# Key search in a sparse-attention mixer: one fp32r pass per head over stacked high and low parts, scored ahead of compression

## Chip, cores and metric

The kernel runs on one core of one Trainium2 chip. The metric is the device time of one execution in microseconds; a comparison takes the median of several runs. The inputs and the output are in the chip's HBM, and everything between is one launch.

## What is computed

Two transformer blocks follow one another on 256 tokens of width 1024. The first is a feed-forward layer, a mixer of two kinds of attention, and a second feed-forward layer. The second block has two layers, each of them feed-forward, hybrid mixer, feed-forward. The hybrid mixer joins three attentions: stick-breaking (SB), NSA (compressed, selected and window keys), and DSA, a sparse attention in which a small index network picks the keys of each query. The change is in that key search:

```
iq = apply_rope(iq, cos_i, sin_i)                 # (S, 8 heads, 32)
ik = apply_rope(ik, cos_i, sin_i)                 # (S, 32), one for all heads
iw = iw * 8 ** -0.5 * 32 ** -0.5                  # (S, 8)
logits = relu(einsum('bthd,bsd->bths', qi, ik))
score = einsum('bths,bth->bts', logits, wi)       # -inf where s > t
_, idx = top_k(score, 64)                         # S // 4
# then softmax attention of each query over the 64 keys found
```

All of it is in fp32, with S = 256 tokens, handled as two halves of 128 (t = 0 and t = 1). Half 0 sees 128 keys, half 1 sees 256. In half 0 the mask of visible keys and the top 64 apply to the same 128 keys.

## The kernel before

**Projections.** Every large product is made of three fp32r passes (`mm3`, L255 to L257): weights and activations are split into a high part (rounded to fp32r) and a low part (the residual), and high x high, high x low and low x high are summed in PSUM. A weight tile of 128 x 1024 is fetched by SP's queue, its high part made by ScalarE (`hi`, L239) and its low part by VectorE (`lo`, L240); there are four buffers of each of `raw`, `hi` and `lo`. One such tile feeds 12 matmuls of 512 columns, six for each half of the tokens.

**Order.** The program is written in order, and a scheduler sets the order on each engine: of what is ready, what stands first in the program goes first, and a tile waits for a free buffer of its tag. Each engine then runs its list in order. In PSUM the tag `mm` has three banks (projections), `at` two (scores of every kind), `tp` two (transposes), `po` one.

**The hybrid mixer (`mixer2`)** runs in this order of program text: SB attention; `ckv`, the projections of NSA keys and values; `nq`, NSA queries; `ix`, the projection of the key search (296 columns: 8 heads x 32 of queries, 32 of keys, 8 weights); `dsaq`, the projection for the sparse attention; `cmp`, the compression of NSA keys and values, whose matmuls (L1189) read weights that lie split in the buffers `gl`; `nsa`, twelve units of NSA attention in a chain of scores, softmax, transposes and values, with the sparse attention of each half behind it; then `gate`, the gate projections (24 weight tiles, 288 matmuls), which write into the same `gl` buffers. The gate projections need nothing of the attentions, so they run as filler from the end of `dsaq` on.

**The key search.** `idx_evac` (L1076) takes each half's projection out of PSUM, applies rope, copies the key part four times beside itself (`kd`), makes three 128 x 128 transposes into one `tp` bank (L1086), and copies the queries (ScalarE, L1087) and keys (VectorE, L1088) to SBUF. `iq` then holds four heads in each of two column blocks, head b of a block on partitions 32b to 32b + 31, and `ik` holds the keys four times, once on each of these strips. `best(t)` (L1121) makes the scores: for each head an fp32 matmul over the 32 partitions of its strip (L1133; each shows as two records in the trace), two heads to an `at` bank, relu on ScalarE (`rl`, L1136), and on VectorE the sum over the heads weighted by `wi` (`iacc`, L1139). Then eight rounds find the eight largest of what is left and mark them (L1144, L1145), and the marks become the mask `M[t]` of the sparse attention.

`best` is a generator: the code of the compression and of the NSA units calls `step(n)`, which runs it on to its next `yield`, so that its parts are woven into theirs. Before, the first `step` (behind the compression's first eight matmuls) issues the scores of half 0 with the first round, and the scores of half 1 come when half 0 is done, among the NSA units.

Of the kernel before, what the change touches and what calls it, by code (L numbers as in the profile page):

```python
# [8 lines left out]
F32 = mybir.dt.float32  # L9
F32R = mybir.dt.float32r  # L10
# [6 lines left out]
P = 128  # L17
S = 256
# [99 lines left out]
class K:  # L118
# [732 lines left out]
    def mixer2(self, l, nxt):  # L851
        nc, tc, d = self.nc, self.tc, self.d
# [6 lines left out]
        with ExitStack() as outer:  # L859
# [3 lines left out]
            T = lambda shape, tag, bufs=1, dt=F32: self.tile(mp, shape, tag, dt, bufs)  # L863
            L = lambda shape, tag, bufs=1, dt=F32: self.tile(kp, shape, tag, dt, bufs)
            toks = [slice(0, P), slice(P, S)]
# [4 lines left out]
            for t in range(2):  # L870
                a = rsv[:, 2 * t:2 * t + 1]
                nc.vector.tensor_scalar(out=a, in0=xs[t][2], scalar1=0.125, scalar2=None, op0=OP.mult)
                b = rsv[:, 2 * t + 1:2 * t + 2]
# [4 lines left out]
            I = T  # L878
# [46 lines left out]
            r = self.rows([G("nsa_q_norm"), G("nsa_k_norm"), G("dsa_q_norm"), G("dsa_k_norm")])  # L925
            r = r.rearrange("p (i d) -> p i d", d=64)
# [17 lines left out]
            for s in range(2):  # L944
                hs = slice(64 * s, 64 * s + 64)
                nsp, zs = [], []
# [23 lines left out]
                for b in range(2):  # L970
                    nc.tensor.matmul(flat(R[b]), self.negl, flat(nsp[b][0]), start=True, stop=False)
                    nc.tensor.matmul(flat(R[b]), cb["identb"], cb[f"smask{b}"][:, :2 * (S - b * P)],
                                     start=False, stop=False)
# [6 lines left out]
                for t in range(2):  # L980
                    for r in range(2):
                        h = 2 * r + s
                        v = lambda b: sbv[b][:, 64 * h:64 * h + 64]
# [85 lines left out]

            self.sec = "ix"  # L1070

            iq = I([P, 2, S], "zs", 2)
            ik = I([P, 2, S], "zs", 2)[:, 0]
            wi = I([P, 2, 8], "wi")
            wi = [wi[:, t] for t in range(2)]

            def idx_evac(t, ps):
                tok = T([P, 296], "tok", 3)
                self.scaled(tok, ps, xs[t][2])
                self.rope(tok[:, :288].rearrange("p (g d) -> p g d", d=32), *cs(t, 8), 4)  # L1080
                nc.vector.tensor_scalar(out=wi[t], in0=tok[:, 288:296], scalar1=0.0625, scalar2=None, op0=OP.mult)
                kd = I([P, 4, 32], "kd", 2)
                nc.vector.tensor_copy(kd, tok[:, 256:288][:, None, :].to_broadcast([P, 4, 32]))
                p = self.tp([P, 3, P])
                for i, v in enumerate((tok[:, 0:P], tok[:, P:2 * P], kd.rearrange("p r d -> p (r d)"))):
                    nc.tensor.transpose(p[:, i], v, self.ident)  # L1086
                nc.scalar.copy(iq[:, :, toks[t]], p[:, 0:2])  # L1087
                nc.vector.tensor_copy(ik[:, toks[t]], p[:, 2])  # L1088

            self.proj(xs, w, 2456, 296, idx_evac)  # L1090
            self.sec = "dsaq"

# [30 lines left out]
            def best(t):  # L1123
                nk = P * (t + 1)
                vis, invis = c["vis"][:, S - nk:], c["invis"][:, S - nk:]
                acc = I([P, nk], f"iacc{t}")
                lgs = [self.at((P, 2, nk)) for _ in range(4)]
                first = True
                for b0 in range(0, 4, 2):
                    for r in range(2):  # L1130
                        for b in range(b0, b0 + 2):
                            bs = slice(32 * b, 32 * b + 32)
                            nc.tensor.matmul(lgs[b][:, r], iq[bs, r, toks[t]], ik[bs, :nk], start=True, stop=True)  # L1133
                    for b in range(b0, b0 + 2):
                        rl = I([P, 2, nk], "rl", 2)
                        nc.scalar.activation(rl, lgs[b], AF.Relu)  # L1136
                        for r in range(2):
                            h = 4 * r + b
                            nc.vector.scalar_tensor_tensor(out=acc, in0=rl[:, r], scalar=wi[t][:, h:h + 1],  # L1139
                                                           in1=invis if first else acc, op0=OP.mult, op1=OP.add)  # L1140
                            first = False
                for r in range(8):
                    m8 = self.sm(8, "m8")
                    nc.vector.max(out=m8, in_=acc)  # L1144
                    nc.vector.match_replace(out=acc, in_to_replace=m8, in_values=acc, imm_value=MARK)  # L1145
                    yield
                nc.vector.scalar_tensor_tensor(out=acc, in0=acc, scalar=MARK, in1=vis, op0=OP.is_equal, op1=OP.mult)
                m = T([P, nk], f"M{t}", 1, BF)
                nc.vector.tensor_scalar(out=m, in0=acc, scalar1=-1.0, scalar2=-NEG, op0=OP.add, op1=OP.mult)
                M[t] = m  # L1150

            side = [best(0), best(1)]

            def step(n):
                keep, self.sec = self.sec, "top"
                for _ in range(n):
                    while side:
                        try:
                            next(side[0])
                            break  # L1160
                        except StopIteration:
                            side.pop(0)
                self.sec = keep
# [3 lines left out]
            p = self.tp([P, 32])  # L1167
# [4 lines left out]
            for v in range(2):  # L1172
# [4 lines left out]
                for a in range(2):  # L1177
# [10 lines left out]
                    for m in range(8):  # L1188
                        nc.tensor.matmul(hp, ox[:, m].rearrange("p i c -> p (i c)"), w1[16 * v + 8 * a + m],  # L1189
                                         start=a == m == 0, stop=a == 1 and m == 7)  # L1190
# [4 lines left out]
                p = self.tp((P, 32))  # L1195
# [8 lines left out]
                if v == 0:  # L1204
# [3 lines left out]
                    kd = I([32, 2, 64], "kd", 2)  # L1208
                    nc.vector.tensor_copy(kd, kc[:32].to_broadcast([32, 2, 64]))
                    p = self.tp((P, 32))  # L1210
# [261 lines left out]
```

## Time and profile before

| what | value |
|---|---|
| median of 3 runs | 1759.06 us (1758.68 to 1761.39) |
| the profiled execution | 1758.43 us |
| its span, first to last instruction | 1756.6 us |
| TensorE busy in the span | 1735.0 us (99%) |
| VectorE busy | 1112.9 us (63%) |
| ScalarE busy | 933.8 us (53%) |
| GpSimd busy | 42.3 us (2%) |
| granted TensorE clock, mean | 0.999 |

Busy times of TensorE cover the whole of each matmul, also the part of it that lies under the next one; the step from the start of one matmul to the start of the next is what a matmul costs in a stream. The names in the trace are tile tags with the section that made them, so `lo_gate` is the low part of a gate weight and `at_top` a bank of key-search scores. Times of the views are counted from the span's start. The first hybrid mixer's part from `ix` to `nsa` lies at about 770 to 900 us, the second's 619 us later.

### The profile page before, as it was taken

Reading aid. Unit: us, or ns where it says so; the run is one execution under the profiler, and the core shown is the slowest. Engines: PE = TensorE matmul, PEld = TensorE weight load, DVE = VectorE, ACT = ScalarE, POOL = GpSimd, SP = SyncE. Lnnn points to the kernel's source line nnn. Section 1 sums busy time; section 2 is a strip of 40 time slices with the busy share of each in tenths; the row PEclk is TensorE's granted clock in tenths of the full one; section 3 lists DMA queues with packets and bytes.
Section 4 is the critical chain, followed back from the end, with each engine's and each line's share of the span. In section 5 each row is a group of like instructions: output and inputs, shape, how many; then the busy total and the mean of one; then the engine's idle time right before and its main releaser. Section 6 shows DMA issues by size and latency. Waiting matters only on the chain.

```text
span 1756.6 us, 22927 instructions
## 1 busy us (share of the span) xinstructions
PE 1735.0 (99%) x8461; PEld 1429.4 (81%) x8467; DVE 1112.9 (63%) x1800; ACT 933.8 (53%) x1458; POOL 42.3 (2%) x77
## 2 busy tenths in 40 slices
PE   9999999999999999999999999999999999999999
PEld 6888787788878888887887888888888877888887
DVE  5555677555565555697886555555556978875553
ACT  5444567544454454676655444444446766554442
POOL 0000200000000000100000000000001000000000
PEclk9999999999999999999999999999999999999999
DMA  8665644466556656554335665666556452357653
GB/s 286 184 190 182 206 133 144 134 190 183 190 180 197 186 182 202 182 151 146 94 108 187 199 190 181 203 180 185 186 193 205 135 160 85 104 172 206 187 183 132
DMA packets 151744, 303.97 MB, mean 173 GB/s; under 512 B 10584, under 2 KB 42368, under 8 KB 151632
## 3 DMA queue, kind: packets, MB, share of 16 engines
q1 hardware_dynamic: 150400, 301.61, 55.9%
q8 instruction: 67, 1.10, 0.3%
q10 hardware_dynamic: 592, 0.53, 0.1%
q0 software_dynamic: 640, 0.37, 0.1%
q14 instruction: 45, 0.37, 0.1%
HBM read 301.41 MB, written 1.05 MB: 172 GB/s over the span
## 4 chain that ended last, share of the span: by engine, by line
PE 90%; DVE 6%; ACT 2%; issue 1%; DMA 1%; POOL 0%; SPq 0%; DVEq 0%; ACTq 0%; POOLq 0%
PE mm_ffn L257 11%; PE mm_ffn L256 11%; PE mm_ffn L255 11%; PE at_ffn L257 9%; PE at_ffn L255 9%; PE at_ffn L256 9%; PE mm_gate L256 2%; PE mm_gate L257 2%; PE mm_gate L255 2%; PE tp_ffn L293 1%; PE po_ffn L293 1%; PE mm_m L255 1%; PE mm_m L257 1%; PE mm_m L256 1%; PE mm_ckv L257 1%
## 5 line engine op out<-in xcount | busy, mean ns | idle before, releaser
L240 DVE TENSOR_TENSOR lo_ffn<-raw_ffn,hi_ffn 128x1024 fp32r<-128x1024 f32 x392 | 478.1, 1225 | 451.5 <-ACT hi_ffn L239 450.1
L239 ACT CAST hi_ffn<-raw_ffn 128x1024 fp32r<-128x1024 f32 x392 | 411.1, 1054 | 499.9 <-PE at_ffn L257 307.0
L255 PE MATMUL mm_ffn<-hi_ffn,xh_ffn 128*128 128x512 f32 x288 | 112.3, 391 | 1.7 <-ACT xh_ffn L337 1.0
L256 PE MATMUL mm_ffn<-lo_ffn,xh_ffn 128*128 128x512 f32 x288 | 112.3, 391 | 1.1 <-DVE lo_ffn L350 1.1
L257 PE MATMUL mm_ffn<-hi_ffn,xl_ffn 128*128 128x512 f32 x288 | 112.2, 390 | 0.0
L256 PE MATMUL mm_ffn<-lo_ffn,ah_ffn 128*128 128x512 f32 x264 | 103.8, 393 | 0.0
L255 PE MATMUL mm_ffn<-hi_ffn,ah_ffn 128*128 128x512 f32 x264 | 103.3, 391 | 0.0
L256 PE MATMUL at_ffn<-lo_ffn,ah_ffn 128*128 128x512 f32 x264 | 103.1, 390 | 0.0
L257 PE MATMUL at_ffn<-hi_ffn,al_ffn 128*128 128x512 f32 x264 | 102.9, 390 | 0.0
L255 PE MATMUL at_ffn<-hi_ffn,ah_ffn 128*128 128x512 f32 x264 | 102.8, 389 | 0.0
L257 PE MATMUL mm_ffn<-hi_ffn,al_ffn 128*128 128x512 f32 x264 | 102.8, 389 | 0.0
L255 PE MATMUL at_ffn<-hi_ffn,xh_ffn 128*128 128x512 f32 x240 | 94.5, 394 | 0.0
L257 PE MATMUL at_ffn<-hi_ffn,xl_ffn 128*128 128x512 f32 x240 | 93.5, 390 | 0.0
L256 PE MATMUL at_ffn<-lo_ffn,xh_ffn 128*128 128x512 f32 x240 | 93.4, 389 | 0.0
L256 PE MATMUL mm_gate<-lo_gate,xh_ffn 128*128 128x512 f32 x192 | 78.5, 409 | 0.0
L257 PE MATMUL mm_gate<-hi_gate,xl_ffn 128*128 128x512 f32 x192 | 77.1, 405 | 0.0
L255 PE MATMUL mm_gate<-hi_gate,xh_ffn 128*128 128x512 f32 x192 | 77.0, 401 | 0.0
L256 PE MATMUL mm_ffn<-lo_ffn,xh_wo 128*128 128x512 f32 x192 | 74.9, 390 | 0.0
L257 PE MATMUL mm_ffn<-hi_ffn,xl_wo 128*128 128x512 f32 x192 | 74.8, 389 | 0.0
L255 PE MATMUL mm_ffn<-hi_ffn,xh_wo 128*128 128x512 f32 x192 | 74.7, 389 | 0.0
L255 PEld LDWEIGHTS mm_ffn<-hi_ffn,xh_ffn 128*128 128x128 f32 x288 | 54.1, 188 | 13.7 <-ACT hi_ffn L348 1.5
L256 PEld LDWEIGHTS mm_ffn<-lo_ffn,xh_ffn 128*128 128x128 f32 x288 | 54.1, 188 | 12.8 <-DVE lo_ffn L350 1.7
(632 smaller groups left out, 3996.6 us busy)
## 6 DMA issues: line engine op xcount, KB each, us to landing
raw_ffn<-in_ffn_w_gu_dram SPq DMA_DIRECT2D x160, 512.0 KB, 3.8
raw_ffn<-in_ffn_w_down_dram SPq DMA_DIRECT2D x132, 512.0 KB, 3.2
raw_gate<-in_w_gate_dram SPq DMA_DIRECT2D x48, 512.0 KB, 3.7
raw_ffn<-in_ffn_w_gate_dram SPq DMA_DIRECT2D x40, 512.0 KB, 3.8
raw_ffn<-in_ffn_w_up_dram SPq DMA_DIRECT2D x40, 512.0 KB, 3.7
raw_m<-in_w_in_dram SPq DMA_DIRECT2D x22, 512.0 KB, 4.2
raw_ffn<-in_ffn_w_gu_dram SPq DMA_DIRECT2D x32, 256.0 KB, 3.3
raw_wo<-in_w_out_dram SPq DMA_DIRECT2D x16, 512.0 KB, 3.4
```

The lines of the kernel that those rows point to most:

```text
L239: self.lasthi = nc.scalar.copy(hi, raw).ins
L240: self.lastlo = nc.vector.tensor_sub(lo, raw, hi.bitcast(F32)).ins
L255: nc.tensor.matmul(out, xh, wh, start=first, stop=False)
L256: nc.tensor.matmul(out, xh, wl, start=False, stop=False)
L257: self.lastmm = nc.tensor.matmul(out, xl, wh, start=False, stop=last).ins
L293: nc.tensor.transpose(p[:, i], src[:, i * P:(i + 1) * P], self.ident)
```

## The change

Queries and keys of the key search are split into high and low parts, like the operands of the projections, and the three products are made in one matmul, by stacking the parts on the contraction rows: on partitions 0 to 31 the query's high part meets the key's high part, on 32 to 63 the query's low part meets the key's high part, and on 64 to 95 the query's high part meets the key's low part. Each head is one fp32r matmul over 96 partitions in place of an fp32 matmul over 32.

To build the stacks, `idx_evac` now copies each group of four heads four times beside itself (`dup`), transposes each head's copies (four transposes to a `tp` bank, one bank for each of two groups), copies all 128 rows to fp32r, and overwrites rows 32 to 63 by the residual. The keys get one transpose and the residual on rows 64 to 95. GpSimd clears rows 96 to 127 of the key tile once. The query tiles take the two `zs` buffers (half 0) and two of the three `P` buffers (half 1), and the keys take the third `P` buffer; `P` is used again by the softmax of the NSA units.

`best` yields once more, behind its scores, and the new loop over `side` runs both halves to that point ahead of the compression. The rounds of the search stay where they were.

```diff
-            iq = I([P, 2, S], "zs", 2)
-            ik = I([P, 2, S], "zs", 2)[:, 0]
+            iq = [[T([P, 4, P], "zs", 2, F32R) for r in range(2)], [T([P, 4, P], "P", 3, F32R) for r in range(2)]]
+            ik = T([P, 2, S], "P", 3, F32R)[:, 0]
+            nc.gpsimd.memset(ik[96:].bitcast(F32), 0.0)
...
-                p = self.tp([P, 3, P])
-                for i, v in enumerate((tok[:, 0:P], tok[:, P:2 * P], kd.rearrange("p r d -> p (r d)"))):
-                    nc.tensor.transpose(p[:, i], v, self.ident)
-                nc.scalar.copy(iq[:, :, toks[t]], p[:, 0:2])
-                nc.vector.tensor_copy(ik[:, toks[t]], p[:, 2])
+                p = self.tp([P, P])
+                nc.tensor.transpose(p, kd.rearrange("p r d -> p (r d)"), self.ident)
+                nc.scalar.copy(ik[:96, toks[t]], p[:96])
+                low = ik[64:96, toks[t]]
+                nc.vector.tensor_sub(low, p[64:96], low.bitcast(F32))
+                for r in range(2):
+                    dup = T([P, 4, 4, 32], "tok", 3)
+                    nc.scalar.copy(dup, tok[:, P * r:P * r + P].rearrange("p (b d) -> p b d", d=32)[:, :, None, :]
+                                   .to_broadcast([P, 4, 4, 32]))
+                    p = self.tp([P, 4, P])
+                    for b in range(4):
+                        nc.tensor.transpose(p[:, b], dup[:, b].rearrange("p r d -> p (r d)"), self.ident)
+                    nc.scalar.copy(iq[t][r], p)
+                    low = iq[t][r][32:64]
+                    nc.vector.tensor_sub(low, p[32:64], low.bitcast(F32))
...
-                            bs = slice(32 * b, 32 * b + 32)
-                            nc.tensor.matmul(lgs[b][:, r], iq[bs, r, toks[t]], ik[bs, :nk], start=True, stop=True)
+                            nc.tensor.matmul(lgs[b][:, r], iq[t][r][:, b], ik[:, :nk], start=True, stop=True)
...
+                yield
                 for r in range(8):
...
             side = [best(0), best(1)]
+            for s in side:
+                next(s)
```

## Rows read from the trace of the kernel before

**Rows 1.** The page: TensorE's busy time, its granted clock in tenths by slice, chain by engine.

```profile
PE 1735.0 (99%) x8461; PEld 1429.4 (81%) x8467; DVE 1112.9 (63%) x1800; ACT 933.8 (53%) x1458; POOL 42.3 (2%) x77
...
PEclk9999999999999999999999999999999999999999
...
PE 90%; DVE 6%; ACT 2%; issue 1%; DMA 1%; POOL 0%; SPq 0%; DVEq 0%; ACTq 0%; POOLq 0%
```

**Rows 2.** Windows of 8 us: start:end, us, then each engine's busy us.

```profile
784.00:792.00 8.00, 8.00 (x38) 6.40 (x38) 7.80 (x26) 5.03 (x12) 0.00 (x0) 1.00 0.72 225
792.00:800.00 8.00, 7.65 (x38) 5.54 (x36) 7.81 (x21) 3.71 (x9) 0.31 (x1) 1.00 0.81 248
800.00:808.00 8.00, 8.00 (x48) 6.36 (x48) 5.28 (x17) 7.55 (x15) 0.31 (x1) 1.00 0.04 16
808.00:816.00 8.00, 8.00 (x46) 6.96 (x45) 6.10 (x30) 7.11 (x11) 0.00 (x0) 1.00 0.70 197
```

**Rows 3.** The window 776 to 799 us, all instructions, columns as above.

```profile
776.00:799.00 23.00, 22.31 (x105) 17.54 (x104) 22.47 (x61) 13.63 (x30) 0.13 (x1) 1.00 0.63 185
```

**Rows 4.** The same window, instructions of tile lo_gate alone (VectorE).

```profile
776.00:799.00 23.00, 8.83 (x22) 4.13 (x22) 9.73 (x8) 1.00 0.63 185
```

**Rows 5.** The same window, instructions of tile mm_gate alone (TensorE).

```profile
776.00:799.00 23.00, 16.04 (x65) 11.83 (x65) 0.00 (x0) 1.00 0.63 185
```

**Rows 6.** Timeline of TensorE: start, us, instruction, count, idle before.

```profile
798.87 1.14 PE L1189 MATMUL at_cmp<-gl_pn,cop_cmp 128*64 128x256 f32 x8 [0.22 <-DVE cop_cmp L1187]
799.94 0.71 PE L1133 MATMUL at_top<-zs_ix,zs_ix 32*128 32x128 f32 x4
...
801.55 0.40 PE L255 MATMUL mm_gate<-hi_gate,xh_ffn 128*128 128x512 f32 x1
801.88 0.71 PE L1133 MATMUL at_top<-zs_ix,zs_ix 32*128 32x128 f32 x4
802.51 0.50 PE L256 MATMUL mm_gate<-lo_gate,xh_ffn 128*128 128x512 f32 x1
802.85 0.40 PE L257 MATMUL mm_gate<-hi_gate,xl_ffn 128*128 128x512 f32 x1
803.08 0.39 PE L255 MATMUL mm_gate<-hi_gate,xh_ffn 128*128 128x512 f32 x1
803.31 0.40 PE L256 MATMUL mm_gate<-lo_gate,xh_ffn 128*128 128x512 f32 x1
...
804.32 0.71 PE L1133 MATMUL at_top<-zs_ix,zs_ix 32*128 32x128 f32 x8
804.96 0.63 PE L1197 MATMUL tp_cmp<-cf_ffn,kd_cmp 64*128 64x32 f32 x4
```

**Rows 7.** Timeline of VectorE, the last copy of the search's keys.

```profile
781.36 0.28 DVE L1088 COPY zs_ix<-tp_ix 128x128 f32<-128x128 f32 x1
```

**Rows 8.** Window 795 to 850 us, instructions of L1133 alone (scores).

```profile
795.00:850.00 55.00, 6.20 (x32) 3.84 (x32) 1.00 0.42 124
```

**Rows 9.** Timeline of TensorE at the sparse attention's first scores.

```profile
846.80 0.65 PE L607 MATMUL at_dsa<-dk_dsaq,dq_dsaq 128*128 128x128 f32 x4
847.29 0.28 PE L615 MATMUL at_dsa<-M_top,cb 128*128 128x256 bf16 x1
```

**Rows 10.** Timeline of TensorE at the second half's index transposes.

```profile
779.36 0.41 PE L1086 MATMUL tp_ix<-ident,tok_ix 128*128 128x128 f32 x2 [0.34 <-DVE qS_nq L1066]
779.61 0.27 PE L1086 MATMUL tp_ix<-ident,kd_ix 128*128 128x128 f32 x1
```

**Rows 11.** Groups by shape, VectorE, 740 to 900 us: count, busy, mean ns.

```profile
L1066 DVE TENSOR_TENSOR qS_nq<-tp_nq,qS_nq 64x512 fp32r<-64x512 f32 x4 | 2.8, 688 | 0.1
```

**Rows 12.** Groups by shape, ScalarE, the same stretch.

```profile
L1318 ACT CAST cop_nsa<-tp_nsa 128x512 fp32r<-128x512 f32 x12 | 7.1, 589 | 3.9 <-PE tp_nsa L1315 3.9
...
L964 ACT CAST rl_sb<-sp_sb 128x512 fp32r<-128x512 f32 x1 | 0.6, 625 | 0.0
```

**Rows 13.** Window 795 to 850 us, instructions of L1139 alone (weighted sums).

```profile
795.00:850.00 55.00, 6.54 (x16) 1.00 0.42 124
```

## The prediction, made before the change was run

> **What bounds the kernel now.** I read the page first, then the stretches of the second block's mixer, then single queues. On the page TensorE is busy for 1735.0 us and the chain that ended last lies on it for 90%; its granted clock is at the upper level, 2.4 GHz, in every slice [rows 1]. So the first question to any edit is how many TensorE microseconds it takes out. The second question comes from the windows: in the stretch in which the changed code stands, about 776 to 799 us in the first of the two mixer layers (the second repeats it 619 us later), VectorE is as full as TensorE: 7.80 and 7.81 of 8 us, against 5.28 and 6.10 in the two slices behind [rows 2], and 22.47 of 23.00 us over the stretch [rows 3].
>
> What the two engines do there matters. VectorE has 9.73 us of the 23 in eight `lo_gate` splits, the residuals of the gate weights [rows 4]. TensorE lives on them: once the last sparse-attention projection is through, it runs 65 gate matmuls [rows 5] until the compression's first matmul at 798.87, which waits 0.22 us for VectorE's `cop_cmp` [rows 6]. A split feeds 12 gate matmuls of 0.23 us (803.08 to 803.31), 2.7 us for TensorE. The reader should see a stretch where TensorE is kept busy by filler that VectorE just manages to make.
>
> The key search's scores start at 799.94 [rows 6], although the last copy of its inputs ran at 781.36 [rows 7]: they stand behind the compression's bank in the order of the `at` tiles. The code after has them ahead of it.
>
> **The change part by part, for one layer; there are two.**
>
> *Scores removed from TensorE behind 799.* The 32 fp32 records (two for a head) hold TensorE for 6.20 us [rows 8]. Each group also breaks the stream: from the gate matmul at 801.55 to that at 802.85 are 1.30 us, of which two steps of 0.23 are the gates' own, so a group of two heads costs 0.84 us where its records cover 0.63 [rows 6]. Six groups, most of them beside other switches, add about 0.6 us. Removed: 6.8 us, from a stretch where TensorE has no idle time to speak of.
>
> *Scores added ahead.* 16 fp32r matmuls. The nearest row is the sparse attention's: four of 128 columns run from 846.80 to 847.29, 0.12 us each [rows 9]; 96 rows for 128 and 256 columns for half of them should not change that much. 1.9 us; bounds 1.6 and 2.5.
>
> The row of eight records at 804.32 takes 0.64 us to the next matmul, the same as four records at 801.88 [rows 6]: four heads in different strips of rows did run in pairs side by side. The Trainium skill ("TensorE: Matmul & The Clock Gate", Part 3, packing small matmuls) says that slices starting at partitions 0, 32, 64 and 96 run concurrently, which speaks against widening them to 96 rows. By that rule alone the old scores would cost four batches, about 3.4 us, and the saving would be 3.4 us smaller; by the rows most heads did not overlap, and 6.8 us stands.
>
> *Preparation, TensorE.* For each token half nine transposes in three PSUM tiles in place of three in one. Two steps take 0.25 us (779.36 to 779.61) [rows 10]: 12 more are 1.5 us, with breaks in the stream 1.7. The second old group waited 0.34 us for a VectorE operation to free its bank [rows 10]; four more tiles pass through the same two banks, so this wait can come again.
>
> *Preparation, VectorE and ScalarE.* Each half gets two residuals of 32x512, which like the 64x512 one take 0.69 us [rows 11]; the 32x128 one is about the old 128x128 copy of 0.28 [rows 7] that it replaces. VectorE: +2.8 us a layer. ScalarE: two copies of 128x512 from SBUF (0.63) and two from PSUM (0.59) [rows 12] in each half and a small one, less an old one: about +4.7 us a layer. ScalarE has room (13.63 of 23 us [rows 3]), but its 4.7 us and the relus lengthen the chain to the compression. I cost that at nothing, since what this chain waits for is mostly VectorE; without that cover it would be up to 2 us. The memset on GpSimd is one instruction, long before its reader, and costs nothing. No DMA is added.
>
> *Scores moved, VectorE.* The 16 weighted sums of a layer take 6.54 us [rows 13], today all behind 799, where VectorE has spare time. They now precede the compression in program order, and the gate splits stand far behind both. So in the full stretch VectorE gets 2.8 + 6.5 = 9.3 us more work that outranks the splits.
>
> *The balance.* The stretch cannot hold it. Either the compression comes later or fewer splits are made. If L of the eight splits (1.22 us each) remain ahead of it, the compression starts 9.3 - 1.2 x (8 - L) us later, and TensorE has had at most 12 L of its 65 gate matmuls; the others must follow later at 0.23 us, behind which TensorE is full. The removed 6.8 us come off. The new transposes and scores cost nothing extra, as they fall into the idle time.
> L = 2: 2.1 + 9.4 - 6.8 = +4.7 us. L = 3: 3.3 + 6.7 - 6.8 = +3.2. L = 4: 4.5 + 3.9 - 6.8 = +1.6. L = 5: 5.7 + 1.2 - 6.8 = +0.1. L = 6: 6.9 + 0 - 6.8 = +0.1.
> Today's splits are made in the gaps of the sparse-attention evacuation's long chain. The sums, short and ready early, fill these gaps first; but they wait for ScalarE's relus and two banks, so some gaps stay. I take 3 to 4: +2.3 us a layer, +4.5 us for both. In the stretch behind, VectorE gets the 6.5 us back, which is worth nothing, as TensorE was full there.
>
> The sum is made against the profiled execution: 1758.43 us, of which 1756.6 are span. The median of the runs is 1759.06, 0.6 us more; 1759.06 + 4.5 gives 1763.5 us.
>
> **The rivals.** *TensorE's own sum decides (faster).* If the sums do not displace the splits, because relus or banks hold them until VectorE has time, then only TensorE's balance counts: 6.8 - 1.9 - 1.7 = 3.2 us a layer, 6.4 in all: 1752.7 us. If the new work also hides entirely, 13.6: 1745.5. For it: 1735.0 us of TensorE in 1756.6. Against it: no free time on VectorE in the stretch. It decides from L above 5 with half of the sums behind the compression's start. Chance 0.30.
>
> *The two cancel.* L = 5 or 6: 0 to +0.3 us: about 1759. For it: the splits ran some 2 us ahead of their use. Chance 0.27, to which belong the cases up to 3.5 us either way.
>
> *The evacuation becomes a chain of its own (slower by more).* Three tiles a half through two transpose banks, each held for a ScalarE copy and a VectorE residual, 0.59 + 0.69, with the sparse attention's transposes queued behind: its token tiles and PSUM banks come free later, so the gates' second and third bank too, and L falls to 2. +4.7 us a layer or, with 1 us of waits, 5.7: 1768.5 to 1770.5. Chance 0.13.
>
> That the fp32r pass isn't cheaper than the fp32 one is excluded by rows 9 against rows 6.
>
> **How the numbers follow.** The forecast, slower by 3.5 to 7 us, has 0.30; with the third rival, slower has 0.43, same 0.27, faster 0.30. About 0.2%, 3.5 us, is what a measurement of this kernel can tell from no change. The range leaves out the end of the first rival's cases and what is worse than the third: 1750 to 1771. The forecast's own range is 1762 to 1766.
>
> **What would show it.** In the profile after: scores of some 0.12 us a matmul between 783 and 797; fewer than eight `lo_gate` splits and fewer than 65 gate matmuls ahead of the compression's first matmul; that matmul 3 to 5 us later than 798.87; TensorE idle, released by VectorE, some 4 to 6 us in that stretch, where it now has under 1; no score records behind it, and VectorE emptier from 800 to 845. If eight splits still precede the compression, it starts by 801 and TensorE has no idle time ahead of it, the balance is wrong and the first rival holds.

## The result, and the profile after

The changed kernel takes 1773.5 us, the median of three runs (1773.3 to 1775.76), against 1759.06: a ratio of 1.0082, 95% interval 1.0068 to 1.0096. It is slower by 14.4 us. 1763.5 had been forecast, with a range up to 1771: the sign was right, the size three times too small.

The page of the kernel after: TensorE's busy time, its granted clock in tenths by slice, the chain by engine (as rows 1).

```profile
PE 1741.7 (98%) x8453; PEld 1435.9 (81%) x8459; DVE 1117.9 (63%) x1808; ACT 942.2 (53%) x1474; POOL 42.9 (2%) x79
...
PEclk9999999999999999998999999999999989999999
...
PE 87%; DVE 8%; ACT 3%; issue 1%; DMA 1%; POOL 0%; SPq 0%; DVEq 0%; ACTq 0%; POOLq 0%
```

TensorE is busy 6.7 us longer than in [rows 1], although it has eight records fewer; about half of that arises in the first 250 us. Two slices have a lower granted clock: one in each hybrid mixer. The windows of the kernel after, columns as in rows 2 (this mixer starts 3.7 us later than in the profile before; the two part in the first 250 us, where the change has no code and the mean granted clock is 0.98 for 0.99):

```profile
792.00:800.00 8.00, 7.77 (x39) 5.74 (x38) 7.76 (x36) 5.23 (x14) 0.00 (x0) 1.00 0.13 47
800.00:808.00 8.00, 3.18 (x17) 2.48 (x16) 7.86 (x26) 4.07 (x9) 0.62 (x2) 0.82 0.00 1
808.00:816.00 8.00, 7.97 (x26) 6.30 (x25) 6.05 (x13) 4.11 (x9) 0.00 (x0) 0.54 0.49 135
816.00:824.00 8.00, 7.88 (x44) 6.50 (x42) 4.21 (x15) 7.03 (x11) 0.00 (x0) 1.00 0.84 257
```

In [rows 2] TensorE has 8.00 of 8 us from 800 on. Here it has 3.18, with VectorE at 7.86, and then 26 matmul records in 7.97 us where there were 46: the clock is 0.54. The timeline of TensorE shows both (start, us, instruction, count, idle before):

```profile
800.64 0.40 PE L1144 MATMUL at_top<-P_ix,P_ix 128*128 128x256 f32 x2
804.62 1.50 PE L1203 MATMUL at_cmp<-gl_pn,cop_cmp 128*64 128x256 f32 x8 [3.58 <-DVE cop_cmp L1201]
807.36 1.97 PE L1203 MATMUL at_cmp<-gl_pn,cop_cmp 128*64 128x256 f32 x8 [1.24 <-DVE cop_cmp L1201]
809.12 0.63 PE L256 MATMUL mm_gate<-lo_gate,xh_ffn 128*128 128x512 f32 x1
...
813.50 0.63 PE L255 MATMUL mm_gate<-hi_gate,xh_ffn 128*128 128x512 f32 x1
813.92 0.63 PE L256 MATMUL mm_gate<-lo_gate,xh_ffn 128*128 128x512 f32 x1
...
815.76 0.40 PE L256 MATMUL mm_gate<-lo_gate,xh_ffn 128*128 128x512 f32 x1
815.99 0.40 PE L257 MATMUL mm_gate<-hi_gate,xl_ffn 128*128 128x512 f32 x1
```

The first compression group waits 3.58 us for VectorE's `cop_cmp` (0.22 in [rows 6]) and the second 1.24. From 805.2 to 815.4 us, and in the second layer from 1429.8 to 1440.0, the granted clock is 0.5, the 1.2 GHz level; a gate matmul then takes 0.42 us from start to start, and 0.23 again from 815.76 on. In the first layer the clock falls 0.6 us behind the end of the long wait, in the second 0.9 us ahead of it; the second wait lies inside the slow stretch. The kernel before has no such stretch in its hybrid mixers. The Trainium skill ("TensorE: Matmul & The Clock Gate", Part 1, on oscillation in real kernels) says that gaps between bursts of matmuls bring the engine back to the lower clock; this trace agrees, with its wait of 3.58 us. E8 and E13 below fall to it with no wait ahead above 1.23 and 1.69 us.

The window that answers to rows 3 to 5, shifted by 3.75 us: all instructions, then those of `lo_gate` and of `mm_gate` alone.

```profile
779.75:802.75 23.00, 20.76 (x106) 15.74 (x104) 22.28 (x72) 18.93 (x44) 0.00 (x0) 1.00 0.30 93
...
779.75:802.75 23.00, 4.84 (x12) 2.27 (x12) 3.58 (x3) 1.00 0.30 93
...
779.75:802.75 23.00, 10.87 (x39) 6.68 (x39) 0.00 (x0) 1.00 0.30 93
```

VectorE is as full as before, with three splits in place of eight [rows 4], and 39 gate matmuls in place of 65 [rows 5].

To see where the time is, I summed TensorE's timeline of the first mixer by tile, as a ledger: from the end of `dsaq` to the first matmul of the branch projections, each matmul counted from its start to the start of the next, without the idle time ahead of that one, which has a row of its own. For a mixer of before, of after, and of the three runs below that decide the question:

```
us of TensorE         before   after   E10 no resid.  E12 resid. first  E13 resid., no bank
idle                    1.4     7.3        3.3             3.3              6.9
scores + transposes     5.7     4.0        3.0             3.5              3.5
gate projections       71.9    74.3       72.7            72.4             74.6
compression             5.7     7.3        5.5             5.6              7.4
all else               34.1    33.8       33.8            34.6             34.0
sum                   118.9   126.7      118.3           119.3            126.3
```

After against before, +7.8 us: idle +5.9; the search's scores and transposes -1.7; gates +2.4 and compression +1.6, mostly the clock: against E10, which has as many gates ahead of the compression and no lower clock, they are +1.6 and +1.8. The second layer gives +6.9: 14.7 in the two profiles, for the 14.4 of the medians.

### The profile page after: what moved, and what is told of

Same layout as the page of the kernel before. It is cut to its first block, busy times and chain, and to the rows that moved or that the text cites. A ratio compares the mean times of both kernels' runs of the same rounds, so it can differ in the third digit from the quotient of the medians.

```text
span 1774.0 us, 22961 instructions
## 1 busy us (share of the span) xinstructions
PE 1741.7 (98%) x8453; PEld 1435.9 (81%) x8459; DVE 1117.9 (63%) x1808; ACT 942.2 (53%) x1474; POOL 42.9 (2%) x79
## 4 chain that ended last, share of the span: by engine, by line
PE 87%; DVE 8%; ACT 3%; issue 1%; DMA 1%; POOL 0%; SPq 0%; DVEq 0%; ACTq 0%; POOLq 0%
PE mm_ffn L257 11%; PE mm_ffn L256 11%; PE mm_ffn L255 11%; PE at_ffn L257 9%; PE at_ffn L255 9%; PE at_ffn L256 9%; PE mm_gate L257 2%; PE mm_gate L256 2%; PE mm_gate L255 2%; PE tp_ffn L293 1%; PE po_ffn L293 1%; PE mm_m L255 1%; PE mm_m L257 1%; PE mm_m L256 1%; PE mm_ckv L255 1%
## 5 line engine op out<-in xcount | busy, mean ns | idle before, releaser
L240 DVE TENSOR_TENSOR lo_gate<-raw_gate,hi_gate 128x1024 fp32r<-128x1024 f32 x48 | 58.2, 1216 | 13.1 <-ACT hi_gate L239 12.8
```

What stands on the lines that cost most here:

```text
L240: self.lastlo = nc.vector.tensor_sub(lo, raw, hi.bitcast(F32)).ins
```

## The experiments

Each run was timed against the kernel before on the same chip (1759.4 to 1759.9 us there). Diffs are against the kernel after unless said. Where the gates, the attentions or the compression are said to come earlier or later, the first mixer is meant, against the kernel before unless said, counted from the mixer's first matmul.

**Order alone (E1).** The kernel before with only the last two hunks of the change: fp32 scores, no stacks, both halves ahead of the compression.

```diff
+                yield
                 for r in range(8):
...
             side = [best(0), best(1)]
+            for s in side:
+                next(s)
```

> The order alone: the kernel before, with its fp32 scores over 32 partitions, but both halves scored ahead of the compression; no stacks, no new transposes. Displacement (the weighted sums ahead of the compression push the gate splits out of VectorE's full stretch, TensorE runs out of gate matmuls, idles and drops to the lower clock): three splits and 39 gate matmuls ahead of the compression as in the changed kernel, a wait of 2 us or more there, a stretch at the lower clock, and 1768 to 1778 us. Preparation (the nine transposes through two banks, with their copies and residuals, make the loss): 1757 to 1762 us, as none of them is here.

1764.8 us, ratio 1.0027 (1.0015 to 1.0039), between the two ranges. 39 gate matmuls stand ahead of the compression, as after, with only the 6.6 us of sums as VectorE's new work. In the profiled execution, the longest of seven (1767.2 us), the gates end 4.5 us later in each layer, and each has a stretch of 3.4 us at the lower clock. By the medians the move alone costs 5.1 us, about a third of the loss.

**Stacks alone (E2).** The stacks and one fp32r pass, scores where they were before (other buffers for the stacks: one of the `gain` pool and `gS`).

```diff
-                yield
...
-            for s in side:
-                next(s)
```

> The stacks alone: fp32r scores over 96 partitions as in the changed kernel, but in the place of before, woven into the compression and the NSA units; the second half's query stacks lie in the buffer of the gain rows and the keys in that of the key gains, so that no softmax buffer is held. Displacement: eight splits ahead of the compression, no wait there of over 1 us, no lower clock; 3 to 7 us faster than before by TensorE's sum (6.8 - 1.9 - 1.7 a layer) if VectorE's 2.8 us a layer hide, so 1750 to 1757 us. Preparation: the loss stays, 1766 to 1774 us.

1766.5 us, 1.0036 (1.0024 to 1.0048): slower than before too, as the rival (preparation) gave. The timeline of TensorE at the end of this mixer shows the last gate matmul, the last values of the sparse attention and the first branch matmul, in the kernel before:

```profile
900.46 0.40 PE L257 MATMUL mm_gate<-hi_gate,xl_ffn 128*128 128x512 f32 x1
897.98 1.89 PE L645 MATMUL po_dsa<-dv_dsaq,rl_dsa 128*128 128x64 f32 x16
900.69 0.39 PE L255 MATMUL mm_br<-hi_br,oTh_gate 128*128 128x512 f32 x1
```

The same three in the kernel after:

```profile
912.02 0.39 PE L257 MATMUL mm_gate<-hi_gate,xl_ffn 128*128 128x512 f32 x1
900.19 1.90 PE L645 MATMUL po_dsa<-dv_dsaq,rl_dsa 128*128 128x64 f32 x16
912.24 0.39 PE L255 MATMUL mm_br<-hi_br,oTh_gate 128*128 128x512 f32 x1
```

And in E2:

```profile
898.62 0.40 PE L257 MATMUL mm_gate<-hi_gate,xl_ffn 128*128 128x512 f32 x1
902.22 2.00 PE L645 MATMUL po_dsa<-dv_dsaq,rl_dsa 128*128 128x64 f32 x16 [0.77 <-DVE ob_nsa L1355]
904.77 0.76 PE L255 MATMUL mm_br<-hi_br,oTh_gate 128*128 128x512 f32 x1 [0.55 <-issue]
```

This I had not seen: in the kernel before the gates and the attentions end within a microsecond of each other, so a mixer ends with the later of two chains. After, 10 us of gates are left when the attentions are done; in E2 the gates are used up and the attentions end 3.5 us later than before. The 288 gate matmuls are a fixed stock of filler, and what counts is how it is spread:

```
gate matmuls          ahead of     to the last  to the last values   behind
                      compression  NSA scores   of the sparse att.
before                    65          192            27            4
after, E1                 39          183            23           43
E10 (no residuals)        39          202            22           25
E12 (residual first)      52          189            22           25
E2 (old place)            72          193            23            0
E7 (E2, no residuals)     62          215            11            0
E4 (behind compr.)        72          216             0            0
```

**Idle time filled (E3).** Sixteen unread bf16 matmuls a layer ahead of the compression's first group, so that TensorE is not idle there.

```diff
+                    if v == 0 and a == 0:
+                        junk = self.po()
+                        wz = self.misc[:, 32:64].bitcast(BF)
...
+                        for _ in range(16):
+                            nc.tensor.matmul(junk[:64], wz, cb["smask0"], start=True, stop=True)
```

> The changed kernel with 16 bf16 matmuls a layer that nobody reads, behind the compression's position rows (their weights are a copy of these rows), to stand in the idle time ahead of the compression. Idle time with the clock (the idle time also costs the drop to 1.2 GHz behind it, some 4.5 us a layer): the granted clock stays at 1.00 and the time falls to 1762 to 1767 us, although TensorE has 32 matmuls more to do. Idle time alone (the drop costs nothing of its own, since VectorE sets the pace there): 1772 to 1776 us.

1769.3 us, 1.0053 (1.0038 to 1.0068), between the two ranges: 4.2 us faster than after, with more work on TensorE. The idle time ahead of the compression falls from 4.0 us to 1.9, not to nothing. The compression starts 1.4 us later than after. The first mixer has no stretch at the lower clock and ends its gates 4.8 us behind before, not 7.8; the second has one of 3.4 us and ends 6.1 behind. The lower clock is a part of the loss, and not all of it.

**Scores behind the compression (E4).** The loop over `side` moved behind the compression's matmuls, and the `step` among these left out.

> The changed kernel with both halves scored behind the compression instead of ahead of it; stacks, buffers and preparation as changed; the rounds of the search that the compression called are left to the NSA units. Displacement: eight splits and 72 gate matmuls ahead of the compression, no lower clock, 1750 to 1758 us. Preparation: 1766 to 1774 us, since the preparation stands where it stood.

1779.8 us, 1.0108 (1.0093 to 1.0123), the slowest of all, against my expectation. The gates end 12.6 us earlier than before and the attentions 9.5 us later: the search is scored from 823.6 us on (799.9 before), the first NSA scores come at 832.1 (823.4 before), and behind the last gate TensorE waits for the NSA units' softmax with no filler left. My first theory, displacement alone, fell with this run and E2.

**Preparation later (E5).** Copies, transposes and residuals moved from the projection's evacuation into `best(t)`, at the old place of the scores.

> Stacks as changed, scores in the place of before, and the preparation (copies, nine transposes, residuals of a half) moved out of the projection's evacuation to just ahead of that half's scores; the search's tokens wait in the buffer of the gain rows. Two bounds (a mixer ends at the later of the last gate matmul and the end of the attentions, and what stands ahead of the compression in VectorE's full stretch delays the latter): the compression starts no later than before, the gates end 3 us a layer earlier, the attentions about where they were; 1752 to 1760 us. Preparation costs wherever it stands (transposes and ScalarE copies now lie in the compression's own chain): 1764 to 1770 us.

1770.4 us, 1.0063 (1.0046 to 1.008), at the upper end of what the rival gave. Gates 12.1 us earlier, attentions 5.0 later: the same trade as E4.

**VectorE's load alone (E6).** The kernel before with two more 128 x 512 products for each half in `idx_evac`, four of 0.69 us a layer, read by nobody.

```diff
+                pad = self.tile(self.gpool, [P, 2, 256], "gain")
+                for _ in range(2):
+                    nc.vector.tensor_mul(pad, tok[:, None, 0:256].to_broadcast([P, 2, 256]),
+                                         tok[:, None, 0:256].to_broadcast([P, 2, 256]))
```

> The kernel before with two more VectorE products of 128x512 in each half of the search's evacuation (some 2.7 us a layer, results unused), and nothing else of the change. If VectorE's time in its full stretch is what the preparation costs: the compression starts 2 to 4 us later in each layer, the attentions end later by as much, 1763 to 1768 us. If it is the transposes, their two banks and ScalarE's copies: 1759 to 1761 us.

1762.5 us, 1.0015 (1.0005 to 1.0024), just below the range for VectorE's time: 1.3 us a layer for 2.7 us. In the profiled execution the compression starts 2.4 us later and the mixers end 1.9 and 1.7 us later, with no lower clock. By the one or the other, VectorE's time in this stretch costs 0.5 to 0.7 of itself. The products also stand ahead of VectorE's copy out of the transposes' bank, so this run doesn't part time from held banks; E13 does.

**E2 without the residuals (E7).** The low parts remain copies of the high ones, so the scores are not the reference's.

> The stacks in the place of before (as in the run with the stacks alone), without the VectorE residuals: the low rows keep the rounded values, so the scores are not those of the reference; all transposes and copies stay. If VectorE's time is what the preparation costs: the compression starts as in the kernel before, 1752 to 1760 us. If transposes, banks and ScalarE's copies: as with the residuals, 1764 to 1768 us.

1767.4 us, 1.004 (1.0025 to 1.0055), no better than E2, as the rival gave. At the old place of the scores the residuals' time doesn't decide: the gates end 10.1 us earlier than before, none of them is left for the attentions' end, and that comes 3.1 us later.

**Four splits first (E8).** The first four gate tiles loaded and split ahead of the early scores; the gate projections then use them.

```diff
...
+            pre = [self.load(G("w_gate"), 2 * P * i, 2, 0, 512) for i in range(4)]
             for s in side:
                 next(s)
...
```

> The changed kernel with the first four gate weight tiles fetched and split ahead of the early scores in program order, so that four splits outrank the weighted sums. If the loss is TensorE without gate matmuls ahead of the compression and the clock that falls for it: 48 or more gate matmuls there, no stretch at the lower clock, 1763 to 1769 us. If it is VectorE's total ahead of the compression, whatever its order: the compression starts later by the splits' 4 to 5 us, 1771 to 1777 us.

1770.8 us, 1.006 (1.0045 to 1.0075), between the two ranges. 49 gate matmuls ahead, idle time ahead of the compression 2.3 us in place of 4.0. It gave an unplanned test of the clock: both layers run one list, with waits for `cop_cmp` of 1.27 and 1.18 us in the first and 1.11 and 1.23 in the second, but only the second fell to the lower clock. TensorE's timeline at these waits in both layers, and the windows around them, columns as in rows 2:

```profile
803.02 1.14 PE L1205 MATMUL at_cmp<-gl_pn,cop_cmp 128*64 128x256 f32 x8 [1.27 <-DVE cop_cmp L1203]
806.17 1.13 PE L1205 MATMUL at_cmp<-gl_pn,cop_cmp 128*64 128x256 f32 x8 [1.18 <-DVE cop_cmp L1203]
...
1425.83 1.11 PE L1205 MATMUL at_cmp<-gl_pn,cop_cmp 128*64 128x256 f32 x8 [1.11 <-DVE cop_cmp L1203]
1428.98 1.97 PE L1205 MATMUL at_cmp<-gl_pn,cop_cmp 128*64 128x256 f32 x8 [1.23 <-DVE cop_cmp L1203]
...
802.00:814.00 12.00, 8.76 (x46) 6.96 (x47) 11.80 (x31) 7.95 (x15) 0.62 (x2) 1.00 0.32 86
1424.00:1436.00 12.00, 8.90 (x34) 6.68 (x34) 10.91 (x33) 7.61 (x14) 0.62 (x2) 0.68 0.18 47
```

The gates end 4.5 us behind before in the first and 7.4 in the second: 2.9 us for 10.2 us at the lower clock. Summed as above, the second layer's gates and compression take 4.0 us longer than the first's, and its idle time is 0.8 us less.

**Half 0 ahead only (E9).** As E2, with the new `yield` and `next` for half 0 alone.

```diff
-                yield
+                if t == 0:
+                    yield
...
-            for s in side:
-                next(s)
+            next(side[0])
```

> Stacks as in the change, but only half 0's scores and sums stand ahead of the compression; half 1's stand where they were before. In the order of the list 49 gate matmuls and four splits precede the compression (65 and eight before, 39 and three after). Theory (displacement sets the gates' end, and the attentions' end is a second bound): displaced gates 16 x 0.23 = 3.7 us, compression some 1 to 2 us later, 6.8 us removed, so the gates end 1 to 2 us before the attentions; no stretch at the lower clock; the attentions end 1 to 3 us later than before and set the time: 1762 to 1766. Rival (the stacks' preparation alone costs 3 us a layer wherever the scores stand): 1766 to 1768, attentions' end 3 to 4 us later. If the gates' end is later than before, the displacement is worse than its count of matmuls says.

1766.4 us, 1.0037 (1.0024 to 1.005). Gates 3.2 us earlier, attentions 3.0 later; the same trade as E2, at the border of what the two theories gave, so it separates nothing.

**After, without the residuals (E10).** Both early halves and all stacks; only the three residuals of each half are left out, so the scores are not the reference's.

```diff
-                low = ik[64:96, toks[t]]
-                nc.vector.tensor_sub(low, p[64:96], low.bitcast(F32))
...
-                    low = iq[t][r][32:64]
-                    nc.vector.tensor_sub(low, p[32:64], low.bitcast(F32))
```

> The changed kernel without its three residuals in each half, so the low parts stay copies of the high ones and the scores are not those of the reference; the order of TensorE's list ahead of the compression is the changed kernel's (39 gate matmuls). Theory (VectorE's work ahead of the compression sets its start): the compression starts up to 2.8 us earlier than in the changed kernel, the stretch at the lower clock is shorter or absent in at least one layer, 2 to 5 us a layer less: 1764 to 1769. Rival (ScalarE's copies and the banks' chain set the start): the compression within 0.7 us of the changed kernel's, 10 us at the lower clock again, 1771.5 to 1774.

1758.7 us, 0.9987 (0.9978 to 0.9997). It is 14.8 us faster than after, where the theory had given 4.5 to 9.5, and no slower than before, though 39 gate matmuls stand ahead of the compression exactly as after. The compression starts 4.0 us earlier than after, and 2.0 earlier than before. The residuals, seen in the profile of after as groups by shape on VectorE (count, busy, mean ns):

```profile
L1100 DVE TENSOR_TENSOR P_ix<-tp_ix,P_ix 32x512 fp32r<-32x512 f32 x2 | 1.4, 684 | 0.1
L1100 DVE TENSOR_TENSOR zs_ix<-tp_ix,zs_ix 32x512 fp32r<-32x512 f32 x2 | 1.3, 678 | 0.0
L1090 DVE TENSOR_TENSOR P_ix<-tp_ix,P_ix 32x128 fp32r<-32x128 f32 x2 | 0.6, 289 | 0.1
```

3.3 us a layer, which cost 7.4. The windows of E10 around the compression:

```profile
776.00:799.00 23.00, 22.12 (x120) 17.50 (x120) 22.39 (x74) 20.18 (x46) 0.31 (x1) 1.00 0.42 138
...
800.00:816.00 16.00, 14.30 (x77) 11.68 (x76) 13.12 (x35) 11.94 (x19) 0.31 (x1) 1.00 0.60 190
```

No stretch at the lower clock, and its first compression group starts without a wait:

```profile
798.37 1.10 PE L1199 MATMUL at_cmp<-gl_pn,cop_cmp 128*64 128x256 f32 x8
```

**Half 0 ahead in fp32 (E11).** The kernel before with E9's two edits.

> The kernel before with only half 0's scores and sums ahead of the compression, in fp32, no stacks; 43 gate matmuls and four splits precede the compression in the list. Theory (displacement): 22 displaced gate matmuls are 5.1 us behind, about 3.2 us of half 0's scores leave that stretch, compression within 1 us of before: gates end +2 a layer, 1761 to 1765, below the 5 us that both halves early cost. Rival (a gain, since the attentions' end, the second bound, gets its first search rounds earlier and the gates still end with it): 1756 to 1758.

1764.6 us, 1.003 (1.0018 to 1.0041): no better than both halves (E1), at the upper end of the theory's range. The rival, a gain, falls.

**Residuals ahead of the transposes (E12).** The same stacks in the same place, but the low part is made from the token layout on all partitions, 128 x 128, in place of 32 x 512 out of the transposes' bank.

```diff
-                    dup = T([P, 4, 4, 32], "tok", 3)
+                    dup = T([P, 4, 4, 32], "tok", 3, F32R)
...
+                    nc.vector.tensor_sub(dup[:, :, 1], tok[:, P * r:P * r + P].rearrange("p (b d) -> p b d", d=32),
+                                         dup[:, :, 1].bitcast(F32))
...
-                    low = iq[t][r][32:64]
-                    nc.vector.tensor_sub(low, p[32:64], low.bitcast(F32))
```

The keys are done alike in `kd`.

> The same stacks and the same place of the scores, but each residual is taken on the token layout, before the transposes, as 128 x 128 (and 128 x 32 for the keys) in place of 32 x 512 behind them: by the widths, about 0.3 us for 0.68, so VectorE gets some 1.9 us a layer less ahead of the compression and no transposes' bank waits for a residual. In the order of the list 52 gate matmuls and five splits precede the compression (39 and three after). Theory (VectorE's time ahead of the compression decides, and past the point at which it is late by more than some 2 us the lower clock comes on top): compression within 2 us of before either way, no stretch at the lower clock, 1755 to 1762. Rival (new work in this stretch costs in proportion): the run without residuals gained 14.8 us for 2.8 us a layer, so 1.9 gains 10: 1763 to 1765.

1760.8 us, 1.0004 (0.9995 to 1.0013): the theory's range. 12.7 us of the 14.4 are gone, and it computes what the changed kernel does. Groups by shape on VectorE in this run:

```profile
L1094 DVE TENSOR_TENSOR tok_ix<-tok_ix,tok_ix 128x128 fp32r<-128x128 f32 x4 | 1.1, 286 | 0.0
L1086 DVE TENSOR_TENSOR kd_ix<-tok_ix,kd_ix 128x32 fp32r<-128x32 f32 x2 | 0.4, 190 | 0.0
```

1.5 us a layer for 3.3. The compression's first group:

```profile
801.77 1.10 PE L1201 MATMUL at_cmp<-gl_pn,cop_cmp 128*64 128x256 f32 x8
```

It starts without a wait, 1.2 us later than before relative to the mixer's first matmul; no lower clock in the first layer, but 3.4 us in the second, where the theory had none.

**Residuals' time without their bank (E13).** Each residual replaced by a product of the same shape that reads the SBUF tile, so that the transposes' bank comes free behind ScalarE's copy; the scores are not the reference's.

```diff
-                    nc.vector.tensor_sub(low, p[32:64], low.bitcast(F32))
+                    nc.vector.tensor_mul(low, low.bitcast(F32), low.bitcast(F32))
```

> The changed kernel with each residual replaced by a VectorE product of the same shape that reads the SBUF tile and not the transposes' bank, so the bank comes free behind ScalarE's copy; the scores are not those of the reference. 39 gate matmuls and three splits precede the compression, as after. Theory (VectorE's time is the price): within 3 us of the changed kernel, 1770 to 1775, with a stretch at the lower clock in both layers. Rival (the held banks are the price): near the run without residuals, 1757 to 1762, and no such stretch.

1772.6 us, 1.0076 (1.0062 to 1.0089): the loss of after, all but 1 us. TensorE's waits in this mixer have one large line (total, times, longest):

```profile
PE at_cmp L1203 <- DVE cop_cmp L1201: 3.1, 2, 1.7
```

The window behind it has the lower clock, 0.68 on the mean:

```profile
800.00:816.00 16.00, 12.98 (x52) 10.61 (x53) 12.44 (x32) 8.03 (x15) 0.62 (x2) 0.68 0.43 123
```

VectorE's microseconds are the cause, not the banks they hold. Nor is it a longer chain of waits to the compression: in the kernel after VectorE is never idle for more than 0.04 us from 771 to 810 us, so what stands ahead of `cop_cmp` on it is work.

## Why the prediction was right in sign and wrong in size

**Which stretch and which engine: right.** VectorE could not hold the new work. Three splits and 39 gate matmuls ahead of the compression are the forecast's L = 3; the sums took 6.6 us (6.5 forecast). Scores run at 0.12 us where they are back to back, and none is left behind the compression. E10, E12 and the kernel after show VectorE's time as the cause: with 0, 1.5 and 3.3 us of residuals a layer they take 1758.7, 1760.8 and 1773.5 us; E13 has the 3.3 us without the held banks and takes 1772.6.

**"The others must follow later at 0.23 us, behind which TensorE is full": the step that failed.** Both halves of it did. The balance had no term for the lower clock. By rows, from the second compression group at 807.36 to 815.5, TensorE takes some 3.5 us more than for the same instructions at full clock (the group 1.76 for 1.07, its four transposes about 1.0 for 0.56, some eleven gate matmuls 0.2 each). By the ledger gates and compression take 4.0 us longer than before and 3.4 longer than in E10; E8's two layers differ by 2.9. At 2.9 to 4.0 us a layer that is 6 to 8 us of the 14.4. And TensorE was not full behind: the second group waited 1.24 us (0.80 in the second layer), `tp_cmp` 1.0 where it had waited 0.5. Put into the forecast's own balance, the measured values give 2.0 us (compression later) + 6.0 (26 gates displaced) - 5.7 (scores removed) = +2.3, the number forecast. The 5.5 us beyond it are 2.2 of idle time behind the compression and some 3.3 of slower matmuls, both put at nothing. That the rest comes out is partly luck: the start of L = 3 was 1.3 us too late and the removal 1.1 us too large, and these offset each other.

**The idle time: forecast 4 to 6 us a layer ahead of the compression, measured 4.0 there (0.35 before) and +5.9 over the mixer.** The compression starts 2.0 us later relative to the mixer, less than the 3.3 of L = 3. The rest of the idle time lies in waits behind it, where the forecast had none.

**The scores removed: 6.8 us forecast, 5.7 measured; less 1.9 and 1.7 for the new ones, 3.2 us of saving a layer forecast, about 2.7 measured.** The 6.20 us of rows 8 are busy time, which counts the part of a matmul that lies under the next one; from start to start the old scores hold 5.7, and no gain from fewer breaks shows in the gates (71.9 before, 72.7 in E10). In E10, at full clock, scores and transposes behind `dsaq` take 3.0 us. After shows only 1.7, with its idle time and breaks around them. The sum by what was measured is +5.9 idle, +4.0 slower gates and compression, -1.7 search, -0.4 of all else and rounding, +7.8; the forecast had +2.3.

**The rivals.** "TensorE's own sum decides" was put at 1752.7. E10 shows that even without the residuals that could not come: of 2.7 us saved a layer 1.9 returned as idle time. "The evacuation becomes a chain of its own" named banks and had the nearest time, 1768.5 to 1770.5, but L stayed at 3, and E13, which frees the banks earlier, refutes its mechanism. ScalarE's longer chain, costed at nothing, was costed rightly: E10 and E12 have it and run as fast as before. That most of the old heads did not overlap is an effect of the order, not of the strips: each group of two heads fills one bank and so lies on one strip, and at 804.32 [rows 6], where two banks were free, two strips ran side by side.

**What the prediction didn't look at.** That gates and attentions end together. E2, E4, E5, E7 and E9 all give TensorE its filler back ahead of time and lose 3 to 10 us a layer at the attentions' end. The place and the load act together: without residuals the early place beats the old one by 8.7 us (E10 against E7), with them it loses by 7.0 (after against E2). Why the lists of those runs spread the filler so much earlier is not settled; the table shows that they do.

No run that computes the reference's scores beats the kernel before; E12 equals it, and E10, which leaves the residuals out, is 0.9 us below it.

## What to carry to other kernels

When an engine is already full in a stretch, don't multiply its new microseconds by one price: here 1.5 us a layer cost 1 us and the next 1.8 cost 6.4 (E10, E12, after; E12's residuals also stand elsewhere in the list), because past the slack TensorE ran dry and its clock fell as well. Price forecast idle time on TensorE with the slower matmuls behind it. And make residuals where they lie on all 128 partitions: the same values cost 0.29 us as 128 x 128 and 0.68 as 32 x 512.

## What the hardware showed unexpectedly

In the kernel after, both layers have 10.2 us at 1.2 GHz that begin within a microsecond of the end of a wait of 3.58 us. But E13 has as much with waits of at most 1.69 us, and in E8 two waits of about 1.2 us, with little work between them, came with it in one layer and not in the other, in the same list of instructions; what decides there stays open. A VectorE operation on two tensors of 32 x 512 took as long with both in SBUF (678 ns, the product of E13) as with one in PSUM (684 and 678 ns, the residuals), and as long as one of 64 x 512 (688 ns, [rows 11]): the partitions left empty save nothing.
